# A fourth Strassen product of gate/up in passes, and one main loop over both halves of the tokens

## The chip, the cores and the metric

The kernel runs on one core of one Trainium2 chip. The time is the device time of one execution in microseconds. TensorE (PE) multiplies, VectorE (DVE), ScalarE (ACT) and GpSimd (POOL) work on elements, and nearly all DMAs are issued in order by SyncE (SP).

## The reference, cut to what matters

One decoder block on 2048 tokens of 1024 channels in float32: attention and pooling with their projections, then a SwiGLU network of inner width 2816. The change concerns the network alone:

```python
h = rmsnorm(x, g_ffn_pre) * (1.0 + scale_f) + shift_f            # (2048, 1024)
f = (jax.nn.silu(h @ w_gate) * (h @ w_up)) @ w_down              # w_gate, w_up: (1024, 2816), w_down: (2816, 1024)
x = x + gate_f * rmsnorm(f, g_ffn_post)
```

## The kernel before, in words

**The arithmetic.** A float32 matrix is split into a high and a low fp32r part, and a product is three matmuls, high·high, low·high and high·low (`mm3`, L66 to L73). The split is a cast on ACT, and a subtraction on DVE (`split`, L59). `split_by_bank` (L1170) has ACT copy the rounded part into a PSUM bank as well, so that DVE's subtraction reads one operand from PSUM and one from SBUF.

**Strassen-Winograd outside.** The 2048 tokens are two halves, sb 0 and 1, of 1024. Within a half, h is a 2 by 2 matrix of blocks (512 channels by 512 tokens), and each of w_gate and w_up is, for each j of 11, a 2 by 2 matrix of 512 by 128 blocks (columns j and j+11). Seven products of block sums take the place of eight. One outer product, for one weight (g or u), one half and one j, is a *step* of 12 matmuls of 512 columns: four slices of channels by three.

**Passes.** Three of the seven products (`NQ = 3`) are computed earlier, in passes. A pass q takes 11 values of j; `inner(q, j)` (L1318) makes a second Strassen over g and u on the one side and the two halves of the tokens on the other, so that the four outer products (g and u, half 0 and 1) take seven inner products of 6 matmuls, 42 instead of 48. The results go to DRAM (`pd`, L1374). Each of the seven is a step of its own. While a pass runs, a generator writes the operands (sums of token blocks, split) of what comes next, one piece for each step: `second_operands` in pass 1, `third_operands` in pass 2, `main_operands` in pass 3. `down_sums` (L1589), placed by `DOWN_AT`, makes the block sums of w_down meanwhile.

**Main loop.** `gate_up(sb, j, at)` (L1537) makes the other four products of g and of u for one half and one j: 8 steps, a *block*. It reads the earlier products back (`px`), adds them up, applies silu and the multiplication, makes the block sums of the result and stores them (`ga`). `matrix` (L1412) loads the weights, makes their sums on POOL and splits them; it does so for each half anew.

**Down.** `down(sb)` (L1730) is a Strassen-Winograd product of the result with w_down for one half: seven phases of 11 chunks, 12 matmuls each. The last phases finish the rows of the output (`p4_end`, `p3_end`). In half 0 the operands of half 1 are made beside it (`token_operands`).

**The order.** All steps stand in one list, made by `halves` (L1983): three passes, main loop of half 0, down of half 0, main loop of half 1, down of half 1. The loop at its end (L2112) goes through it: for step n it first does what is due `ahead` of steps to come (loads, weight sums), then the matmuls, then what is due after earlier steps (`takes`), then splits for steps to come (`split_up_to`: at most `PAIRS = 6` steps from n on), then one piece of the side generator. Each engine runs its instructions in the order in which they are written here.

PSUM banks rotate: `g_ps` has 5 for the products of the main loop. `ring` holds 5 pairs of split operands, `fx` one more.

Of the kernel before, what the change touches and what calls it, by code (L numbers as in the profile page):

```python
# [9 lines left out]
F32 = mybir.dt.float32  # L10
# [36 lines left out]
def block_kernel(ctx, tc, x, c, w_cond, b_cond, g_mix_pre, g_mix_post, w_in, w_pool,  # L47
# [46 lines left out]
    sd = {kind: dt(f"sd{kind}", [P, 4, TB]) for kind in "gu"}  # L94
# [34 lines left out]
    def modulated_t(pool, new_ps, xs, a, b, name):  # L129

        for half in range(2):
# [4 lines left out]
            h32 = ft("tr", f"{name}_h{half}", (P, 4, P)) if pool is fx else pool.tile([P, 4, P], F32, tag="h32", bufs=8 if pool is op else 4, name=f"{name}_h{half}")  # L136
# [1022 lines left out]
    def operand(name):  # L1159
        used[0] += 1  # L1160
        pool = fx if fx is not None and used[0] % (RB + 1) == 0 else ring
        return [pool.tile([P, TB], F32R, tag=f"w{n}", bufs=1 if pool is fx else RB, name=f"{name}_{n}") for n in "hl"]

    def new_ops(pool, sb, names):
        return {n: (pool.tile([P, HK, TB], F32R, tag=f"{n}h", bufs=1, name=f"{n}h{sb}"),
                    pool.tile([P, HK, TB], F32R, tag=f"{n}l", bufs=1, name=f"{n}l{sb}")) for n in names}

    MAIN = ("t2", "t3", "t1", "b22")
# [132 lines left out]
    class Step:  # L1301
        def __init__(self, pairs, split, mm, take=()):
            self.pairs, self.split, self.mm, self.take, self.ahead = pairs, split, mm, list(take), []

# [13 lines left out]
    def inner(q, j):  # L1318
# [6 lines left out]
        def load():  # L1325
            turn = 0 if m == 1 else (NQ * HF - 2 - m) % 4
            if m == 0:
                st["g"], st["u"], st["s12"], st["s34"] = (t[:, n] for t in raw_pair(ring, name, (P, 2, TB)) for n in range(2))
            else:
                if m == NQ * HF - 1:  # L1330
                    w = opools["0b"].tile([P, 4, TB], F32, tag="y22", bufs=1, name=f"{name}_32")
                else:
                    w = raw_tile(ring if turn > 1 else fx, turn % 2 == 0, name, (P, 2, TB))
                st["g"], st["u"] = w[:, 0], w[:, 1]
            for n, src in (("g", w_gate), ("u", w_up)):
                (nc.scalar if m in (4, 5) else nc.sync).dma_start(st[n].rearrange("p (k n) -> p k n", k=HK), rows_of(src, min(q, 1) * HK, j + q // 2 * HF))
# [36 lines left out]
        def keep(kind, sb, t):  # L1373
            nc.sync.dma_start(pd[sb][:, j, 2 * q + kind, :], t)  # L1374
# [34 lines left out]
        r[0].ahead = [({1: 9, 2: 12}.get(m, 14), load), (5 if m == 1 else 8, s12), (4 if m == 1 else 7, s34)]  # L1409
        return r  # L1410

    def matrix(kind, src, sb, j, at, take):  # L1412

        name = f"{kind}{sb}_{j}"
        st = {}
        turn_back = sb == 1 and at == 0
        SUMS = ("s2", "s3", "s1", "s4")

        def load(i):
            f = j + i * HF  # L1420
            w32 = raw_tile(ring if kind == "g" else fx, i, name, (P, KC, P))
            if turn_back:
                nc.scalar.dma_start(w32.rearrange("p (i k) n -> p i (k n)", i=2), sd[kind][:, 2 * i:2 * i + 2, :])
                st[SUMS[2 * i]], st[SUMS[2 * i + 1]] = (w32[:, k:k + HK, :].rearrange("p k n -> p (k n)") for k in (0, HK))
                return
            nc.sync.dma_start(w32, rows(src)[:, :, f * P:(f + 1) * P])
            st[("a11", "s1")[i]], st[("a12", "a22")[i]] = (w32[:, k:k + HK, :].rearrange("p k n -> p (k n)") for k in (0, HK))

        def load0():
            load(0)  # L1430

        def load1():
            load(1)
# [727 lines left out]
```

## Time and profile before

| what | value |
|---|---|
| median of 3 runs | 2219.2 us (2216.96 to 2219.46) |
| the profiled execution | 2218.68 us, span 2216.9 us |
| PE busy | 2187.9 us of the span |
| granted TensorE clock, mean | 0.997 |
| DMA, mean over the span | 230 GB/s |
| first half's main loop starts | 1302.49 us (first row of `t_g<-t2h,g_s_h`) |
| down of half 0 | 1543.77 to 1753.37 us |
| main loop of half 1 starts | 1753.21 us |
| down of half 1 | 1999.52 to 2209.12 us |

A row of the timeline has start, duration, engine, line, operation, what is written from what, and in brackets how long the engine was idle before it and what ended that. Names come without their numbers: `t_g<-t2h,g_s_h` is a matmul of the main loop, t2's high part with the split sum of w_gate. A matmul of 512 columns is listed with some 0.39 us, while the next one starts 0.23 us after it: they overlap in the pipeline, so starts are to be compared. Rows of the windows view give, for a stretch, how long each engine was busy and with how many instructions, then the granted clock, the busy share of the DMA engines and their GB/s.

### The profile page before, as it was taken

What the parts mean: (1) busy time and instruction counts of PE and PEld (TensorE: products, weight loads), DVE (VectorE), ACT (ScalarE), POOL (GpSimd) and SP (SyncE); (2) the same over time, 40 slices, a digit from 0 to 9 for tenths busy, and PEclk for the clock granted to TensorE, in tenths of its full rate; (3) what the DMA queues carried; (4) which work ended last, traced back from release to release, by engine and by line L of the source; (5) the groups of instructions that cost most, each with busy time, mean ns of one, the idle gap of its engine ahead of it and who ended that gap; (6) DMA issues with size and microseconds to landing.
All of it is one profiled execution on the core that took longest, in us unless ns stands there. A gap on an engine that the chain in (4) does not pass through costs nothing.

```text
span 2216.9 us, 34775 instructions
## 1 busy us (share of the span) xinstructions
PE 2187.9 (99%) x10415; PEld 1809.8 (82%) x10415; DVE 1692.0 (76%) x2555; ACT 1411.6 (64%) x2879; POOL 1241.8 (56%) x1694
## 2 busy tenths in 40 slices
PE   8999999999999999999999999999999999999998
PEld 6888888888888888888888888888888878888887
DVE  7874499999999966557788877878676777876566
ACT  5334599989989855457666666665554556664444
POOL 1352277787779965548888737774120477761003
PEclk9999999999999999999999999999999999999999
DMA  9996886534444456669989877878777888868664
GB/s 316 335 289 211 283 209 183 161 91 119 119 125 114 135 176 195 199 224 303 316 298 324 283 267 240 274 250 285 271 236 215 257 288 275 261 228 311 208 191 150
DMA packets 385000, 510.66 MB, mean 230 GB/s; under 512 B 25190, under 2 KB 223402, under 8 KB 381868
## 3 DMA queue, kind: packets, MB, share of 16 engines
q1 hardware_dynamic: 381676, 504.77, 70.8%
q10 hardware_dynamic: 3136, 3.67, 0.6%
q8 instruction: 83, 1.36, 0.3%
q14 instruction: 105, 0.86, 0.1%
HBM read 345.29 MB, written 163.05 MB: 229 GB/s over the span
## 4 chain that ended last, share of the span: by engine, by line
PE 54%; DVE 2%; issue 1%; POOL 1%; ACT 1%; DMA 1%; DVEq 0%; SPq 0%; POOLq 0%; ACTq 0%
PE dn0p L72 3%; PE dn0p L73 3%; PE dn0p L71 3%; PE dn1p L71 3%; PE dn1p L72 3%; PE dn1p L73 3%; PE t_g L71 2%; PE t_g L72 2%; PE t_g L73 2%; PE t_u L73 2%; PE t_u L72 2%; PE t_u L71 2%; PE mix L71 1%; PE mix L73 1%; PE mix L72 1%
## 5 line engine op out<-in xcount | busy, mean ns | idle before, releaser
L953 POOL TENSOR_TENSOR w<-sg,pr 128x512 f32<-128x512 f32 (+2 forms) x320 | 306.3, 957 | 46.4 <-DVE pr L948 15.2
L948 DVE TENSOR_TENSOR_SCAN pr<-pr,carry,begin 128x512 f32<-128x512 f32 x192 | 244.2, 1272 | 0.0
L932 ACT ACTIVATE sg<-z 128x512 f32<-128x512 f32 (+2 forms) x320 | 183.0, 572 | 50.9 <-PE z L930 41.1
L62 DVE TENSOR_TENSOR wtl<-wt,wth 128x512 fp32r<-128x512 f32 (+1 forms) x320 | 189.9, 593 | 17.8 <-ACT wth L61 15.7
L61 ACT CAST wth<-wt 128x512 fp32r<-128x512 f32 (+1 forms) x320 | 181.8, 568 | 10.4 <-PE wt L964 8.0
L934 ACT ACTIVATE pr<-z 128x512 f32<-128x512 f32 (+2 forms) x320 | 182.1, 569 | 0.0
L964 PE MATMUL wt<-ident,w 128*128 128x128 f32 x1088 | 172.3, 273 | 1.5 <-POOL pr L944 1.1
L964 PEld LDWEIGHTS wt<-ident,w 128*128 128x128 f32 x1088 | 134.1, 140 | 32.7 <-POOL pr L944 1.8
L979 PE MATMUL av<-wth,vt 128*128 128x512 f32 (+1 forms) x320 | 126.1, 394 | 0.9 <-ACT o L984 0.8
L71 PE MATMUL dn0p<-w0p_h,g0p_h 128*128 128x512 f32 x308 | 119.8, 389 | 0.0
L72 PE MATMUL dn0p<-w0p_l,g0p_h 128*128 128x512 f32 x308 | 119.8, 389 | 0.0
L73 PE MATMUL dn0p<-w0p_h,g0p_l 128*128 128x512 f32 x308 | 119.8, 389 | 0.0
L929 PE MATMUL z<-kt,qt 128*128 128x512 f32 (+2 forms) x320 | 118.7, 371 | 0.7 <-ACT pr L934 0.6
L980 PE MATMUL av<-wtl,vt 128*128 128x512 f32 (+1 forms) x320 | 117.8, 368 | 1.3 <-DVE wtl L62 1.2
L930 PE MATMUL z<-kt,qt 128*128 128x512 f32 (+2 forms) x320 | 117.0, 366 | 0.0
L71 PE MATMUL dn1p<-w1p_h,g1p_h 128*128 128x512 f32 x292 | 113.6, 389 | 0.0
L72 PE MATMUL dn1p<-w1p_l,g1p_h 128*128 128x512 f32 x292 | 113.6, 389 | 0.0
L73 PE MATMUL dn1p<-w1p_h,g1p_l 128*128 128x512 f32 x292 | 113.6, 389 | 0.0
L945 DVE TENSOR_TENSOR_SCAN pr<-pr,zero,begin 128x128 f32<-128x128 f32 (+3 forms) x128 | 111.3, 872 | 1.7 <-ACT pr L934 1.7
L61 ACT CAST g0p_h<-g0p 128x512 fp32r<-128x512 f32 x77 | 48.0, 623 | 100.6 <-PE dn0p L72 82.8
L62 DVE TENSOR_TENSOR g1p_l<-g1p,g1p_h 128x512 fp32r<-128x512 f32 x73 | 52.6, 721 | 74.4 <-ACT g1p_h L61 73.7
L1567 POOL TENSOR_TENSOR gs<-s,s 128x512 f32<-128x512 f32 x44 | 57.8, 1313 | 92.2 <-DVE s L1557 89.2
(808 smaller groups left out, 7298.0 us busy)
## 6 DMA issues: line engine op xcount, KB each, us to landing
pd<-p_c SPq DMA_DIRECT2D x132, 256.0 KB, 4.7
g<-in_w_gate_dram SPq DMA_DIRECT2D x42, 512.0 KB, 5.2
u<-in_w_up_dram SPq DMA_DIRECT2D x42, 512.0 KB, 5.6
px<-pd SPq DMA_DIRECT2D x11, 1536.0 KB, 9.4
wc<-in_w_cond_dram SPq DMA_DIRECT2D x32, 512.0 KB, 7.6
qt<-qd SPq DMA_DIRECT2D x64, 256.0 KB, 4.1
hs<-h2d SPq DMA_DIRECT2D x60, 256.0 KB, 3.9
kt<-kd SPq DMA_DIRECT2D x96, 128.0 KB, 3.3
```

Source lines behind the costliest of these rows:

```text
L61: nc.scalar.copy(hi, src)
L62: low.tensor_tensor(lo, src, raw(hi), ALU.subtract)
L71: nc.tensor.matmul(ps, lh, rh, start=first and i == 0, stop=False)
L72: nc.tensor.matmul(ps, lh, rl, start=False, stop=False)
L73: nc.tensor.matmul(ps, ll, rh, start=False, stop=last and i == n - 1)
L929: nc.tensor.matmul(z[:, 0:L], qt[:, 0, i * P:(i + 1) * P], keys, start=True, stop=False)
L932: nc.scalar.activation(sg[:, 0:L], z[:, 0:L], AF.Sigmoid, scale=0.125)
L934: nc.scalar.activation(pr[:, 0:L], z[:, 0:L], AF.Sigmoid, scale=-0.125)
L948: nc.vector.tensor_tensor_scan(keys, keys, begin, carry, ALU.mult, ALU.bypass)
L953: nc.gpsimd.tensor_tensor(w[:, 0:L], sg[:, 0:L], pr[:, 1:L + 1], ALU.mult)
L964: nc.tensor.transpose(wt[:, i * P:(i + 1) * P], wss[u][i][:, b * P:(b + 1) * P], ident)
L979: nc.tensor.matmul(av[:, lo0:], vb, wh[:, lo0:], start=first, stop=False)
```

## The change

`NQ` is 4: a fourth outer product, of the sum of the weights' two lower blocks, is computed in a fourth pass. Its weights have to be added first, so that twice as many are loaded, and POOL adds them (`row_sum`). A generator `fourth_operands` makes its token operands in pass 3.

The main loop has three products left for g and for u. It goes over j once: a block is now 12 steps, each of the three products for g and u and for both halves, and half 1 uses the same split weights as half 0. All token operands of half 0 and t2 of half 1 are made in pass 4 (`main_operands`), t3 and b22 of half 1 in the first steps of the loop (`rest_operands`); for that the first block has its steps in another order. The early products come back as four loads of 1 MB for each j (`products_load`), in three buffers.

Down of half 1 follows down of half 0 directly; `switch`, `back`, `token_operands` and the storing of weight sums (`sd`) go. Down loads w for four chunks at once.

```diff
-FT = {"tr": 4, "gs": 3, "u4": 1, "gf": 1, "sr": 4, "s": 6, "u2": 2, "w320": 1, "u3": 2, "w321": 1, "p1": 1, "cu": 2}
-PAIRS, HELD = 6, 4
+FT = {"tr": 1, "gs": 3, "u4": 1, "gf": 1, "sr": 4, "s": 6, "u2": 2, "w320": 1, "u3": 2, "w321": 1, "p1": 1, "cu": 2}
+WIDE = {"tr": 4, "gf": 2, "w320": 2, "w321": 2}
+PAIRS, MAIN_PAIRS, HELD = 6, 4, 4
-NQ = 3
-DOWN_AT = (10, 22, 34, 46, 58, 82, 106, 130, 156, 176, 196)
+NQ = 4
+DOWN_AT = (10, 26, 42, 58, 74, 106, 130, 156, 172, 188, 204)
...
+            k0, f = ((0, j), (HK, j), (HK, j + HF), (0, j + HF))[q]
...
+            if q == 3:
...
+                    w = raw_tile(ring, 1, f"{name}_2", (P, 2, TB))
+                    st["g2"], st["u2nd"] = w[:, 0], w[:, 1]
+                for n, src in (("g2", w_gate), ("u2nd", w_up)):
+                    nc.sync.dma_start(st[n].rearrange("p (k n) -> p k n", k=HK), rows_of(src, HK, f))
+
+        def row_sum(n, other):
+            nc.gpsimd.tensor_tensor(st[n], st[n], st[other], ALU.add)
...
+        if q == 3:
+            r[0].ahead += [(10, lambda: row_sum("g", "g2")), (9, lambda: row_sum("u", "u2nd"))]
...
+    def products_load(n, sb, j):
+
+        tag, pool = (("yah", "0r"), ("yal", "0r"), ("y22", "0b"))[next(px_turn) % 3]
+        px[n, sb, j] = opools[pool].tile([P, 4, TB], F32, tag=tag, bufs=1, name=f"px{n}{sb}_{j}")
+        nc.sync.dma_start(px[n, sb, j], pd[sb][:, j, 4 * n:4 * n + 4])
...
+        def take_p6(kind, sb, ps):
+            p1, p2 = to_bank(0, kind, 0, sb), first(0, kind, 1, sb)
+            u2 = st["u2", kind, sb] = ft("u2" if kind == "g" else "u3", f"u2{kind}{sb}_{j}")
+            nc.vector.tensor_tensor(u2, ps, first(0, kind, 0, sb), ALU.add)
+            if kind == "g":
+                gate("a11", sb, "sr", p1, p2)
+            else:
+                up("a11", sb, p1, p2)
...
+            r = Step(int(make), (lambda: split_w(n)) if make else (lambda: None), mm,
+                     [(late, lambda: after(kind, sb, st["ps", n, kind, sb]))])
+            r.cap, r.takes_first, r.pair = MAIN_PAIRS, True, (n, kind)
+            return r
+
+        order = [(n, sb) for n in ("s2", "s3", "s4") for sb in range(2)]
+        if not at:
+            order = [("s2", 0), ("s2", 1), ("s3", 0), ("s4", 0), ("s3", 1), ("s4", 1)]
+        order = [(n, kind, sb) for n, sb in order for kind in "gu"]
...
     def rest_operands():
 
-        ops["b22"] = pair_of(opools["0"], "ya", "b22")
...
+        ops[1].update({n: pair_of(opools["0b"], tag, f"{n}_1") for n, tag in (("t3", "v14"), ("b22", "v32"))})
...
+        for k in range(HK + 2):
+            if k < HK:
+                nc.gpsimd.tensor_tensor(b12[k], b22[k], b12[k], ALU.subtract)
+            for n, raw, i in (("t3", b12, k - 1), ("b22", b22, k - 2)):
+                if 0 <= i < HK:
+                    put(ops[1][n], slice(i * P, (i + 1) * P), raw[i], split if n == "b22" else split_by_bank)
             yield
...
                 def load_w():
-                    ph["w", j] = t = ft("tr", f"w{name}")
-                    nc.sync.dma_start(t, src[:, j, :])
+                    m = min(4, HF - held - j)
+                    k = next(w_turn) % 3
...
+                    nc.sync.dma_start(t[:, 0:m], src[:, j:j + m, :])
...
-                s.ahead.append((5, load_w))
+                if j % 4 == 0:
+                    s.ahead.append((8 if begin else 5, load_w))
...
-            at[(second_operands, third_operands, main_operands)[q]] = len(r)
+            at[(second_operands, third_operands, fourth_operands, main_operands)[q]] = len(r)
...
+        for j in range(HF):
+            s = gate_up(j, j)
...
         for sb in range(2):
-            for n in range(HF):
-                s = gate_up(sb, (n - 1) % HF if sb else n, n)
...
             d = down(sb, lambda sb=sb: pools[sb])
...
-        while split_to < len(steps) and sum(s.pairs for s in steps[n:split_to + 1]) <= PAIRS:
+        while split_to < len(steps) and sum(s.pairs for s in steps[max(0, n - 12):split_to + 1] if s.last >= n) <= steps[split_to].cap:
```

Three places show how instructions move. On PE, where down of half 0 ends: `dn0p3` is the last phase of half 0, `w0p3` and `g0p3` its operands, `t2_g1_10` the first product of half 1's main loop, `dn1p1` the first phase of down of half 1. Before:

```order
L71 MATMUL dn0p3_3_21359<-w0p3_10_h_21607,g0p3_10_h_21603 128x512
L72 MATMUL dn0p3_3_21359<-w0p3_10_l_21608,g0p3_10_h_21603 128x512
L73 MATMUL dn0p3_3_21359<-w0p3_10_h_21607,g0p3_10_l_21604 128x512
L71 MATMUL t2_g1_10_21673<-t2h1_19634,g1_10_s2_h_21628 128x512
L72 MATMUL t2_g1_10_21673<-t2l1_19635,g1_10_s2_h_21628 128x512
L73 MATMUL t2_g1_10_21673<-t2h1_19634,g1_10_s2_l_21629 128x512
```

And now:

```order
L72 MATMUL dn0p3_3_23427<-w0p3_10_h_23665,g0p3_10_h_23661 128x512
L73 MATMUL dn0p3_3_23427<-w0p3_10_l_23666,g0p3_10_h_23661 128x512
L74 MATMUL dn0p3_3_23427<-w0p3_10_h_23665,g0p3_10_l_23662 128x512
L72 MATMUL dn1p1_0_23734<-w1p1_0_h_23692,g1p1_0_h_23688 128x512
L73 MATMUL dn1p1_0_23734<-w1p1_0_l_23693,g1p1_0_h_23688 128x512
L74 MATMUL dn1p1_0_23734<-w1p1_0_h_23692,g1p1_0_l_23689 128x512
```

The turn from down to a main loop is gone; down meets down.

On DVE, in the middle of a block of the main loop: rows with `_l` are splits of weights, `u2`, `u3`, `u4` are sums of products, `s` the gated results. Before, block j=5 of half 0:

```order
L1457 TENSOR_TENSOR u2g0_5_18303<-t2_g0_5_18254,px0_5_18012 128x512
L1542 TENSOR_TENSOR s0_5_00_18305<-p0g0_5_18244,px0_5_18012 128x512
L1182 TENSOR_TENSOR u0_5_s1_l_18308<-u0_5_s1_18193,rounded_18310 128x512
L1457 TENSOR_TENSOR u3g0_5_18333<-t3_g0_5_18289,u2g0_5_18303 128x512
L1542 TENSOR_TENSOR s0_5_10_18335<-p2g0_5_18283,u3g0_5_18333 128x512
L1182 TENSOR_TENSOR u0_5_s4_l_18338<-u0_5_s4_18218,rounded_18340 128x512
L1457 TENSOR_TENSOR u4g0_5_18359<-t1_g0_5_18315,u2g0_5_18303 128x512
L1542 TENSOR_TENSOR s0_5_11_18361<-t1_g0_5_18315,u3g0_5_18333 128x512
L1182 TENSOR_TENSOR g0_6_s2_l_18364<-g0_6_s2_18285,rounded_18366 128x512
```

And now, block j=5, with `t20`, `t21` the products of half 0 and 1:

```order
L1490 TENSOR_TENSOR u2g0_5_20023<-t20_g_5_19981,px00_5_19792 128x512
L1478 TENSOR_TENSOR sa110_5_20025<-b0g0_5_20021,px00_5_19792 128x512
L1490 TENSOR_TENSOR u2u0_5_20047<-t20_u_5_20007,px00_5_19792 128x512
L1482 TENSOR_TENSOR b0u0_5_20045<-b0u0_5_20045,px00_5_19792 128x512
L1483 TENSOR_TENSOR sa110_5_20025<-sa110_5_20025,b0u0_5_20045 128x512
L1490 TENSOR_TENSOR u2g1_5_20067<-t21_g_5_20030,px01_5_19847 128x512
L1478 TENSOR_TENSOR sa111_5_20069<-b0g1_5_20065,px01_5_19847 128x512
L1177 TENSOR_TENSOR g_5_s4_l_20072<-g_5_s4_19877,rounded_20074 128x512
L1490 TENSOR_TENSOR u2u1_5_20099<-t21_u_5_20051,px01_5_19847 128x512
L1482 TENSOR_TENSOR b0u1_5_20097<-b0u1_5_20097,px01_5_19847 128x512
L1483 TENSOR_TENSOR sa111_5_20069<-sa111_5_20069,b0u1_5_20097 128x512
L1177 TENSOR_TENSOR u_5_s4_l_20104<-u_5_s4_19911,rounded_20106 128x512
```

Before, every third row here is a split of weights; now one in six, and what stands between adds up products. From one `u2g0_5` to the next `u2g0_6` it was 26 rows for 8 steps, and is 40 rows for 12.

On POOL, in the last pass: `p3_5` and `p4_5` are j=5 of the pass, `s12` and `s34` the inner sums of its weights, `hs` the token sums made beside it, `wd` those of w_down. Before, pass 3:

```order
L1348 TENSOR_TENSOR p3_5_s12_16217<-p3_5_321_16111 128x256
L1349 TENSOR_TENSOR p3_5_s12_16217<-p3_5_s12_16217,p3_5_321_16111 128x256
L1353 TENSOR_TENSOR p3_5_s34_16237<-p3_5_321_16111 128x256
L1354 TENSOR_TENSOR p3_5_s34_16237<-p3_5_321_16111,p3_5_s12_16217 128x256
L1586 TENSOR_TENSOR wd9_512_16149<-wd20_512_16153,wd9_512_16149 128x512
```

And now, pass 4:

```order
L1342 TENSOR_TENSOR p4_5_320_17373<-p4_5_320_17373,p4_5_2_321_17376 128x512 x2
L1354 TENSOR_TENSOR p4_5_s12_17515<-p4_5_320_17373 128x256
L1355 TENSOR_TENSOR p4_5_s12_17515<-p4_5_s12_17515,p4_5_320_17373 128x256
L1356 TENSOR_TENSOR p4_5_s34_17529<-p4_5_320_17373 128x256
L1357 TENSOR_TENSOR p4_5_s34_17529<-p4_5_320_17373,p4_5_s12_17515 128x256
L1685 TENSOR_TENSOR hs0_3_1_17471<-hs0_3_3_17473,hs0_3_1_17471 128x512
L1685 TENSOR_TENSOR hs0_3_0_17493<-hs0_3_1_17471,hs0_3_0_17493 128x512
```

Two sums of 512 columns stand ahead of the inner sums, and none of w_down's are left beside them.

More of the change, by code (lines that the diff above doesn't have):

```diff
@@ L1688, in main_operands @@
         for i in range(HK):
-            cols = slice(i * P, (i + 1) * P)
-            done, coming = [], list(order) if i + 1 < HK else []
-            sums = itertools.islice(combine(nc.gpsimd, raw[i, 0], raw[i, 1], None, raw[i, 3]), 3)
-            for at, (n, t) in enumerate(itertools.chain(sums, [(None, None)] * 2)):
-                if done:
-                    put(*done.pop(), split_by_bank)
-                if n:
-                    done.append((ops[n], cols, t))
-                if at > 1 and coming:
-                    load(i + 1, coming.pop(0))
+            now = nxt
```

383 lines of the change are left out of this document (179 added, 204 removed).

## The prediction, made before the result was known

> **What bounds the kernel now.** I read the page first: the engines' shares, the slices, and the chain that ended last.
>
> ```profile
> PE 2187.9 (99%) x10415; PEld 1809.8 (82%) x10415; DVE 1692.0 (76%) x2555; ACT 1411.6 (64%) x2879; POOL 1241.8 (56%) x1694
> ...
> PE   8999999999999999999999999999999999999998
> ...
> PE 54%; DVE 2%; issue 1%; POOL 1%; ACT 1%; DMA 1%; DVEq 0%; SPq 0%; POOLq 0%; ACTq 0%
> ```
>
> PE is busy in every slice, and more than half of the chain is PE; nothing else has over 2%. But busy time hides small losses where matmuls overlap, so I went to the timeline, PE's rows in the first main loop, and compared starts.
>
> ```profile
> 1312.01 0.39 PE L71 MATMUL t_u<-t2h,u_s_h 128*128 128x512 f32 x1
> ...
> 1319.94 0.39 PE L73 MATMUL t_u<-t1h,u_s_l 128*128 128x512 f32 x1
> ```
>
> These are the first and last of 36 matmuls: 7.93 us over 35 distances, 0.2266 us each. A step of 12 is 2.72 us, a block of 8 steps 21.76 us. So a matmul saved is worth 0.2266 us, not the 0.39 us of its row. Then I looked for stretches in which starts are further apart. In the network there is one: the turn from down of half 0 to the main loop of half 1.
>
> ```profile
> 1753.21 0.39 PE L71 MATMUL t_g<-t2h,g_s_h 128*128 128x512 f32 x1
> ...
> 1784.04 0.47 PE L71 MATMUL b_g<-b22h,g_s_h 128*128 128x512 f32 x1 [0.75 <-DVE s L1557]
> ...
> 1801.97 0.57 PE L71 MATMUL t_g<-t2h,g_s_h 128*128 128x512 f32 x1 [3.76 <-DVE s L1542]
> ...
> 1814.56 0.39 PE L71 MATMUL t_u<-t2h,u_s_h 128*128 128x512 f32 x1
> ```
>
> The first row starts a block and the last one stands two and a half blocks later: 61.35 us against 2.5 x 21.76 = 54.40, so **6.95 us** are lost here. What PE waits for is DVE (in brackets), which is late with the products' sums. The windows of the main loop and of down quoted further on have PE busy throughout: the network is bound by PE, and DVE is the engine next to it. How near, the first main loop shows, where DVE starts late and catches up.
>
> ```profile
> 1304.98 0.39 PE L73 MATMUL t_g<-t2h,g_s_l 128*128 128x512 f32 x1
> ...
> 1308.24 0.69 DVE L1457 TENSOR_TENSOR u2g<-t_g,px 128x512 f32<-128x512 f32 x1
> ...
> 1314.50 0.39 PE L73 MATMUL t_u<-t2h,u_s_l 128*128 128x512 f32 x1
> ...
> 1320.17 0.39 PE L71 MATMUL b_g<-b22h,g_s_h 128*128 128x512 f32 x1
> 1320.83 0.50 PE L72 MATMUL b_g<-b22l,g_s_h 128*128 128x512 f32 x1 [0.27 <-DVE b22l L1182]
> ...
> 1322.97 0.68 DVE L1457 TENSOR_TENSOR u2u<-t_u,px 128x512 f32<-128x512 f32 x1
> ...
> 1334.67 0.68 DVE L1457 TENSOR_TENSOR u2g<-t_g,px 128x512 f32<-128x512 f32 x1
> ...
> 1439.07 0.68 DVE L1457 TENSOR_TENSOR u2g<-t_g,px 128x512 f32<-128x512 f32 x1
> ```
>
> A product whose last matmul ends at 1305.37 (1304.98 + 0.39) is taken at 1308.24: a lag of 2.9 us. The next such pair has 8.1 us (1314.89 to 1322.97); meanwhile PE loses 0.4 us (two starts 0.66 apart). The last two rows are five blocks apart, 104.40 us: 20.88 us a block while DVE is behind, against PE's 21.76. Its 26 instructions of a block, with their waits for ACT, take 96% of PE's time. That is the margin to watch.
>
> **The change part by part.** *Fewer matmuls.* A pass computes for one j in 42 matmuls what the main loop does in 48. A fourth pass of 11 values of j saves 66; the matmuls of the built kernel are 66 fewer. 66 x 0.2266 = **-14.95 us**.
>
> *The turn goes.* No main loop follows down of half 0 any more, so the 6.95 us have no place: **-6.95 us**. What is late next is asked at the two new seams below.
>
> *The fourth pass.* A j takes 42 x 0.2266 = 9.52 us. POOL has two sums of 512 and four of 256 columns for it, and 16 token sums of 512 in all 11.
>
> ```profile
> L1586 POOL TENSOR_TENSOR wd<-wd,wd 128x512 f32<-128x512 f32 x22 | 28.4, 1296 | 0.6
> ...
> L1348 POOL TENSOR_TENSOR p_s<-p 128x256 f32<-128x256 f32 x19 | 14.2, 745 | 10.4 <-DVE p_s_l L1182 10.4
> ...
> 1000.00:1104.00 104.00, 102.91 (x457) 85.06 (x456) 78.33 (x131) 74.08 (x143) 87.72 (x97) 1.00 0.94 311
> 1326.00:1541.00 215.00, 215.00 (x950) 178.11 (x949) 169.51 (x266) 137.13 (x241) 144.20 (x113) 1.00 0.78 259
> ```
>
> 2 x 1.30 + 4 x 0.745 + 16 x 1.30 / 11 = 7.5 us, 79% of 9.52; in the first pass POOL is busy 87.7 of 104 us and PE loses little. The weights' second half has one buffer, so that load and sums alternate: 5.5 us to land (row of `p<-in_w_up` below) and 2.6 us of sums make 8.1 us, under 9.52. I take 0; had a load the 7.9 us of the larger row below, 10.5 us would cost 11 x 1.0 = 11 us.
>
> *The main loop.* A block is 12 steps, 32.64 us. DVE has 40 instructions in it. At the pace of the old loop's catching up (20.88 / 26 = 0.803 us each, waits included) they take 32.1 us, 98%. Most of those waits were for ACT's rounded copies, of which there are now 6 in 40 rows and not 8 in 26, so I expect nearer 30. I take 0 for the steady loop. POOL has 16 sums, 16 x 1.30 = 20.8 us of 32.64. DMA: 2 MB of weights, four products' loads of 1 MB and 14 stores of 256 KB are 9.96 million bytes, 305 GB/s; the first window above ran at 311 with a share of 0.94.
>
> *The seam into the main loop.* The new first block has twice the splits of token operands, 8 against 4. From its third step to its eighth I count 31 DVE instructions, 31 x 0.685 = 21.2 us (its rows have 0.68 and 0.69), in 6 x 2.72 = 16.3 us: the lag grows by 4.9 us. If it enters with the old 2.9 us, it reaches 7.8, and some more with waits for ACT. A product may wait four steps, 10.9 us, for its bank is written again by the fifth product after it; at the old turn the loss came at such lags. The nearest rows are the old start of this loop (8.1 us of lag, 0.4 us lost) and the turn (6.95). I take **+1.5 us**, ends 0 and 6.95.
>
> *The seam between the down stages.* Half 0's last rows are finished beside the first splits of half 1. Inside down the same stands between its last two phases, and the row of that stretch has PE busy throughout:
>
> ```profile
> 1706.00:1753.00 47.00, 47.00 (x209) 38.91 (x209) 36.03 (x50) 25.74 (x51) 18.02 (x15) 1.00 0.83 263
> 1753.00:1815.00 62.00, 57.44 (x244) 46.50 (x243) 45.90 (x70) 33.05 (x61) 42.09 (x35) 0.97 0.84 269
> ...
> 1734.57 1.74 POOL L1836 TENSOR_TENSOR y_v<-y_v,gf 128x512 f32<-128x512 f32 x1
> 1735.09 1.78 DVE L62 TENSOR_TENSOR g0p_l<-g0p,g0p_h 128x512 fp32r<-128x512 f32 x1
> 1736.79 0.68 DVE L62 TENSOR_TENSOR w0p_l<-w0p,w0p_h 128x512 fp32r<-128x512 f32 x1
> ```
>
> A split that meets a POOL sum takes 1.78 us in place of 0.68. Four rows with two POOL operations each could cost DVE 8 x 1.1 = 8.8 us there. The stretch above has just these and loses nothing, since splits run two chunks (5.4 us) ahead. I take 0, ends 0 and 6.95 (what the turn lost). The Trainium skill, "SBUF — State Buffer", section "SBUF: two separate sides", says that a VectorE operation with two SBUF inputs and a GpSimd operation lock each other out of a shared pair of ports, the later one for all of the other's time. That rule speaks against this change, which takes the finishing of rows from beside sums that read PSUM to beside splits that read SBUF twice; by it alone the seam would cost DVE the 8.8 us, by the row of the stretch they are covered.
>
> *Larger loads in down.* Four chunks of w come in one load of 1 MB, asked for five chunks ahead.
>
> ```profile
> px<-pd SPq DMA_DIRECT2D x11, 1024.0 KB, 7.9
> ...
> p<-in_w_up_dram SPq DMA_DIRECT2D x31, 256.0 KB, 5.5
> ```
>
> Landing after 7.9 us it meets the split, due three steps (8.2 us) later, and PE two steps after that: 0, with at most some tenths of a us in each of 14 phases.
>
> **The sum** on the profiled execution's 2218.68: -14.95 - 6.95 + 1.5 = 2198.28; that execution lies 0.5 us below the median of the runs, so **2198.8 us**.
>
> **The rivals.** *A seam takes the turn's place.* DVE's lag at the start of the new main loop, or the locked splits between the down stages, stop PE as the turn did. For it: the two counts above; against it: the old start of the loop and the old phase boundary. One seam at the turn's price in place of my 1.5: 2204.2; both: 2211.2.
>
> *DVE becomes the bound of the main loop*, the one that ends slower. Its place is the steady block: if 40 instructions need more than 32.64 us, PE waits in each of 11 blocks. In the stretch of the turn DVE did 70 instructions in 62 us, 0.886 each; at that pace 40 take 35.4 us, 2.8 too many, 11 x 2.8 = 30.8 us, 2228 us. It is slower than before from 35.0 us a block (26 us lost). For it: 96% in the old loop, 98% by the same pace; against it: fewer splits with their waits for ACT.
>
> *DMA becomes the bound of the main loop.* If it gave no more than the old loop's 259 GB/s, a block would take 9.96 / 0.259 = 38.5 us, 11 x 5.8 = 64 us more, 2261. Against it: 311 GB/s in the first pass with 102.91 of 104 us of PE.
>
> *The pass doesn't give what it should*, since load and sum of its weights alternate in one buffer: 11 us as worked out, 2209.8.
>
> **How the numbers follow.** My forecast has 0.60, a seam 0.17, DVE 0.13, DMA 0.06, the slow pass 0.04. The range takes in the forecast with both ends of its unknown costs, the seams and the slow pass: from 2194.5 (no new loss, 2197.3, less the 2.2 us by which the fastest run lies under the median, and a little) to 2211.5 (both seams). It leaves out what DVE or DMA would cost, 0.19. About 0.2%, 4.4 us, is what a measurement of this kernel can tell from no change. Faster by more is the forecast, the seams, the slow pass and a quarter of the DVE and DMA cases: 0.86; within it 0.05; slower 0.09, the rest of DVE and DMA.
>
> **What would show it.** Right: 66 matmuls fewer, starts 0.2266 us apart through passes and main loop, no bracket at the start of `dn1p`, and a lag of `u2g` after its product that falls from block to block. Wrong in the seam: brackets on PE naming DVE in the first block of the loop, or a gap within 30 us after down of half 0. Wrong in the loop: blocks over 32.64 us apart with a lag that stays near 10 us (DVE), or `u2` rows idle until `px` lands, and a DMA share near 1 (DMA). Wrong in the pass: `p4` steps over 9.52 us apart for one j, POOL idle until the weights land.

## The result and the profile after

| | before | after |
| --- | --- | --- |
| median of the runs, us | 2219.33 (4 runs, 2216.96 to 2219.46) | 2233.64 (4 runs, 2231.36 to 2235.74) |
| profiled execution, us | 2218.68 | 2234.14 |
| its span, us | 2216.9 | 2232.4 |

The kernel became slower: the ratio is 1.0067, with a 95% interval of 1.0049 to 1.0084. The forecast was 2198.8, with a range up to 2211.5.

The page of the kernel after has these lines in the places of those shown before: busy time by engine, PE's 40 slices, and the chain that ended last.

```profile
PE 2180.1 (98%) x10349; PEld 1794.5 (80%) x10349; DVE 1669.8 (75%) x2552; ACT 1356.4 (61%) x2796; POOL 1217.4 (55%) x1700
...
PE   8999999999999999999999998799999999999998
...
PE 45%; DMA 4%; DVE 4%; POOL 2%; issue 2%; ACT 2%; SPq 0%; DVEq 0%; POOLq 0%; ACTq 0%
```

The 66 matmuls are gone (10415 to 10349). But PE's slices have a dent in the middle, and the chain, which was 54% PE and 1% DMA, is now 45% PE and 4% DMA. The windows give the dent a place: busy time of PE, PEld, DVE, ACT and POOL, then the granted clock, the DMA share and GB/s.

```profile
1305.00:1431.00 126.00, 111.65 (x466) 86.42 (x464) 82.25 (x136) 67.61 (x127) 78.28 (x80) 0.99 0.72 233
1431.00:1476.00 45.00, 35.62 (x148) 28.75 (x149) 28.16 (x46) 23.40 (x41) 19.82 (x16) 0.89 0.85 297
1476.00:1803.00 327.00, 326.92 (x1443) 270.36 (x1442) 262.95 (x411) 159.52 (x283) 197.65 (x156) 1.00 0.94 310
```

The first row is the fourth pass, the second the first block of the main loop, the third its ten other blocks. By starts of matmuls the stages took:

| stage | at PE's pace | after | lost |
| --- | --- | --- | --- |
| passes 1 to 3 | 317.74 (as before the change) | 322.09 | 4.35 |
| pass 4, 11 x 9.52 | 104.7 | 125.7 | 21.0 |
| first block of the main loop, with a step left over from the pass | 34.0 | 45.3 | 11.3 |
| ten further blocks of 32.64 | 326.4 | 326.8 | 0.4 |
| down of half 0, to the first matmul of half 1 | 209.4 | 209.4 | 0.0 |
| down of half 1, to its last matmul | 209.2 | 211.5 | 2.3 |

The losses are 39.3 us in all. Against them stand 14.95 for the matmuls, 6.95 for the turn, 0.4 that the old start of the loop had lost, and 1.3 by which the part ahead of the passes happened to be shorter; that leaves 15.7, and the two executions are 15.5 apart. So both gains came as worked out. No engine is short of time: in pass 4 DVE is busy 82 of 126 us, POOL 78, DMA 0.72. Something stands. The view of waits for 1306 to 1420 (who stood, for whom; us in total, times, longest) names the waits.

```profile
DVE p_c L1384 <- DMA pd<-p_c: 26.5, 9, 5.3
...
POOL p L1342 <- DMA p<-in_w_up_dram: 10.5, 4, 6.0
...
PEld ap L72 <- ACT rounded L1176: 9.7, 7, 2.3
```

SP's waits are an answer of their own, in the same window:

```profile
SPq L1339 <- POOL p L1342: 33.8, 8, 6.5
```

SP issues nearly all transfers, one after the other, and stands 33.8 us in front of the second weights' loads (L1339) until POOL's row sums (L1342) free the one buffer. Behind these loads in SP are the stores of products (L1380), and DVE stands 26.5 us at `p_c`, which needs a buffer that a store has to empty. SP's timeline shows one turn:

```profile
1341.22 0.38 SPq L1339 DMA_DIRECT2D p<-in_w_gate_dram  x1
1341.65 0.50 SPq L1339 DMA_DIRECT2D p<-in_w_up_dram  x1
...
1346.96 0.63 SPq L1615 DMA_DIRECT2D hs<-h2d  x1
1354.16 0.38 SPq L1339 DMA_DIRECT2D p<-in_w_gate_dram  x1
...
1355.18 0.86 SPq L1380 DMA_DIRECT2D pd<-p_c  x2
...
1359.59 0.67 SPq L1339 DMA_DIRECT2D p<-in_w_up_dram  x1
...
1366.30 0.38 SPq L1339 DMA_DIRECT2D p<-in_w_gate_dram  x1
```

From 1347.59 to 1354.16 SP issues nothing. In that time POOL waits for weights, sums, and so lets SP go on:

```profile
1352.86 1.28 POOL L1342 TENSOR_TENSOR p<-p,p 128x512 f32<-128x512 f32 x1 [2.56 <-DMA p<-in_w_up_dram]
...
1364.97 1.31 POOL L1342 TENSOR_TENSOR p<-p,p 128x512 f32<-128x512 f32 x1 [1.44 <-DMA p<-in_w_up_dram]
```

One j takes 12.1 us (1354.16 to 1366.30): 5.4 us pass between the two loads in SP's queue, since stores and other loads stand between them, 5.4 us until the second has landed (1364.97), 1.3 us of sum. The forecast had 8.1 for the same loop, with both loads going out at once. In the kernel's text they stand one right after the other (L1338 and L1339); the rows of SP show that the built program has SP's transfers in an order of its own. So what is said further up, that each engine runs its instructions in the order in which they are written, doesn't hold for SP.

The first block's loss is one gap. DVE's and PE's rows there:

```profile
1441.24 0.69 DVE L1478 TENSOR_TENSOR sa<-b0g,px 128x512 f32<-128x512 f32 x1
1452.06 0.69 DVE L1384 TENSOR_TENSOR p_c<-dp,u4p 128x512 f32<-128x512 f32 x1 [10.13 <-DMA pd<-p_c]
...
1452.90 0.77 PE L72 MATMUL t_g<-t_0h,g_s_h 128*128 128x512 f32 x1 [9.11 <-DVE p_c L1384]
```

and SP's:

```profile
1432.43 4.88 SPq L1380 DMA_DIRECT2D pd<-p_c  x1
1437.36 6.27 SPq L1615 DMA_DIRECT2D hs<-h2d  x5
...
1444.79 1.66 SPq L1380 DMA_DIRECT2D pd<-p_c  x1
```

`rest_operands` takes four of the six `s` buffers for token parts just when the last products of the pass need them; its loads stand in SP until stores have emptied these buffers, the next store stands behind the loads, and DVE stands 10.13 us for that store.

### The profile page after: what moved, and what is told of

It reads as the page before. It is cut to its first block, busy times and chain, and to the rows that moved or that the text cites. A ratio compares the mean times of both kernels' runs of the same rounds, so it can differ in the third digit from the quotient of the medians.

```text
span 2232.4 us, 34290 instructions
## 1 busy us (share of the span) xinstructions
PE 2180.1 (98%) x10349; PEld 1794.5 (80%) x10349; DVE 1669.8 (75%) x2552; ACT 1356.4 (61%) x2796; POOL 1217.4 (55%) x1700
## 4 chain that ended last, share of the span: by engine, by line
PE 45%; DMA 4%; DVE 4%; POOL 2%; issue 2%; ACT 2%; SPq 0%; DVEq 0%; POOLq 0%; ACTq 0%
PE dn0p L72 3%; PE dn0p L74 3%; PE dn0p L73 3%; DMA pd<-p_c 3%; PE dn1p L73 2%; PE dn1p L74 2%; PE dn1p L72 2%; PE t_u L74 2%; PE t_u L73 2%; PE t_u L72 2%; PE t_g L73 2%; PE t_g L72 2%; PE t_g L74 2%; PE mix L72 1%; PE mix L74 1%
## 5 line engine op out<-in xcount | busy, mean ns | idle before, releaser
L1479 ACT ACTIVATE sa<-sa 128x512 f32<-128x512 f32 x88 | 54.9, 633 | 166.0 <-DVE sa L1478 162.6
L63 DVE TENSOR_TENSOR g0p_l<-g0p,g0p_h 128x512 fp32r<-128x512 f32 x77 | 59.3, 771 | 80.0 <-ACT g0p_h L62 80.0
```

What stands on the lines that cost most here:

```text
L63: low.tensor_tensor(lo, src, raw(hi), ALU.subtract)
```

## The experiments

Times are of the profiled execution of each kernel unless a ratio is given; stages are by starts of matmuls, as in the table above. Where nothing else is said, the edit is made to the kernel after the change. A time without a ratio is that of one execution; ten executions of e10 span 2211.86 to 2218.39 us and five of e17 2204.18 to 2214.36, so single executions don't tell totals apart that differ by a few us.

**Three ways at the one buffer.** *e1_sums_apart*: the row sum reads the first weights twice, so that no sum waits for a second load and no second load for a sum. Loads and sums remain; the block sum of the weights is left out, so its products are not those that are wanted.

```
-            nc.gpsimd.tensor_tensor(st[n], st[n], st[other], ALU.add)
+            nc.gpsimd.tensor_tensor(st[n], st[n], st[n], ALU.add)
```

> As the change, but POOL's two sums of a j in pass 4 add a tile to itself and read nothing of the second half of the weights, which is still loaded: the same loads, the same sums, no load that waits for a sum (the block sum of the weights is left out). Theory (the one buffer: the load waits for the sums, SP waits in front of it, and the stores of products behind it come late): pass 4 goes from 125.8 us to 105 to 108 us; the first block of the main loop from 45.3 to 34 to 38 us; in all 2200 to 2208 us. Rival (pass 4 has too much DMA traffic or too much POOL work): pass 4 stays at 120 us or more, in all 2228 us or more.

*e2_pool_queue*: the loads go out from POOL's queue, behind POOL's own sums.

```
-                    nc.sync.dma_start(st[n].rearrange("p (k n) -> p k n", k=HK), rows_of(src, HK, f))
+                    nc.gpsimd.dma_start(st[n].rearrange("p (k n) -> p k n", k=HK), rows_of(src, HK, f))
```

> As the change, but the second half of pass 4's weights is asked for from POOL's queue, behind the sum that frees the buffer, and not from SP's. Theory (what costs is SP standing in front of that load while stores of products wait behind it, and the two loads being torn apart by other DMAs): pass 4 at 106 to 114 us, in all 2203 to 2218 us. Rival (the latency of load and sum in one buffer is itself too long, whoever issues): pass 4 stays near 125 us.

*e3_split_wait*: the buffer is taken once for the whole pass, so that the load of g waits for the sum of g alone.

```
+    second = {}
...
-                    w = raw_tile(ring, 1, f"{name}_2", (P, 2, TB))
+                    w = second.setdefault(0, None)
+                    if w is None:
+                        w = second[0] = raw_tile(ring, 1, f"{name}_2", (P, 2, TB))
```

> As the change, but the one buffer of the second weights is taken once for the whole pass, so that each of its two halves is loaded as soon as its own sum is done, and not both sums. Theory: the loop for one half is 5.3 us of load and 1.3 us of sum, SP stands shorter; pass 4 at 106 to 118 us, in all 2203 to 2222 us. Rival (traffic or POOL's work): pass 4 stays at 120 us or more.

| | us | pass 4 | first block |
| --- | --- | --- | --- |
| after | 2234.14 | 125.7 | 45.3 |
| e1_sums_apart | 2223.91 | 114.4 | 46.4 |
| e2_pool_queue | 2221.39 | 111.7 | 46.8 |
| e3_split_wait | 2230.46 | 121.2 | 46.0 |

With the same bytes, e1 saves 11.3 us of pass 4 and e2 14.1: what the loads stand for, and whose queue they stand in, costs more than what they carry. Splitting the wait in two gives only 4.5, for SP still stands (36.3 us in its view of waits, 33.8 before). e2 came where its expectation had the pass, e1 and e3 did not (e3's 121.2 is what its rival had), and all missed their expected totals: the first block kept its loss, which I had not seen as a cause of its own. The Trainium skill, "DMA: Bandwidth & Descriptors", section "Rules for kernel authors", says that spreading transfers over several issuing engines doesn't help bandwidth and saves only issue time. By that alone e2 should have won little. Its 12.8 us are not bandwidth: the DMA share was 0.72 in the pass it mends. They are the waits of others behind a load that cannot start, and the loads go out together again: in e2 0.76 us apart, and the loop takes 9.92 us.

```profile
1335.28 0.76 POOL L1339 DMA_DIRECT2D p<-in_w_gate_dram  x1 [0.29 <-POOL p L1342]
1336.04 0.75 POOL L1339 DMA_DIRECT2D p<-in_w_up_dram  x1
...
1345.20 0.76 POOL L1339 DMA_DIRECT2D p<-in_w_gate_dram  x1 [0.29 <-POOL p L1342]
```

What bounds that loop now is POOL's own work: it is busy 9.45 of these 9.92 us, with two row sums, four block sums, two token sums and two issues, and waits for no other engine in it. The loop stays at 9.8 to 9.9 us for five j in a row, over PE's 9.52. What follows is the same fault once more: SP stands up to 9.6 us for a buffer that POOL's token sums free, the first weights stand behind that, and POOL stands 4.6 us for them.

**The stores, and the buffers of the first block.** *e4_stores_act* takes the stores out of SP's queue, *e5_both_queues* does so and has the loads on POOL's, *e8_sr_tags* changes two buffers in `rest_operands` only, and *e9_all_three* does all of it.

```
-            nc.sync.dma_start(pd[sb][:, j, q // 2 * 4 + 2 * kind + q % 2, :], t)
+            nc.scalar.dma_start(pd[sb][:, j, q // 2 * 4 + 2 * kind + q % 2, :], t)
```

```
-        b12 = [token_part(1, NTS, "s", i) for i in range(HK)]
+        b12 = [token_part(1, NTS, tag, i) for i, tag in enumerate(("sr", "sr", "s", "s"))]
```

> The stores of the passes' products (L1380) are issued from ACT's queue, all else as after the change. Theory (SP serves its queue in order, and what stands behind a load that waits for a buffer is late: stores, and so the six `s` buffers, and so DVE): DVE's waits for `pd<-p_c` go (26.5 us from 1306 to 1420 before), the weights' own loop of 12.1 us a j stays; pass 4 falls from 125.8 to 115-122 us, the first block of the main loop from 45.3 to 36-41, the whole to 2218-2228. Rival (the DMA engines are full there, whichever queue issues): pass 4 stays at 123 or more, the block at 44 or more, 2230-2236.

> The second weights' loads (L1339) from POOL's queue, as before, and the products' stores (L1380) from ACT's. Theory: nothing that waits for POOL's sums stands ahead of the stores any more; pass 4 106-111 us (111.7 with the loads alone moved, 104.7 at PE's pace), first block of the main loop 36-41 (46.8), the whole 2205-2214. Rival (what is left after the loads were moved is DMA traffic or DVE's splits): 2218-2224, block 45 or more.

> Two of the four loads of token parts at the start of the main loop go to `sr` buffers in place of `s`, so that four `s` buffers in place of two are left for the last products; all else as after the change. Theory (the first block's 11.3 us are DVE standing at `p_c` for a buffer whose store is behind these loads): first block 45.3 to 35-40, pass 4 as it is, 122-128, the whole 2225-2230. Rival (the block loses its time to the twice as many splits on DVE, as I counted in the prediction, or to the loads of products): block 44-47, 2232-2237.

> All three edits together: second weights' loads from POOL's queue, stores from ACT's, two token parts in `sr`. Theory: pass 4 105-111, first block 34-38, the whole 2202-2211, faster than before by 0.4 to 0.8%. Rival (traffic or DVE): 2217 or more, no faster than before.

| | us | passes 1 to 3 | pass 4 | first block |
| --- | --- | --- | --- | --- |
| e4_stores_act | 2276.76 | 377.1 | 118.0 | 38.3 |
| e5_both_queues | 2267.53 | 378.0 | 112.0 | 37.2 |
| e8_sr_tags | 2225.07 | 320.9 | 125.7 | 38.4 |
| e9_all_three | 2264.13 median, 1.0204 [1.0187, 1.0222] | 375.6 | 113.5 | 34.0 |

In pass 4 and the first block e4 did what the theory said (118.0 and 38.3). But it lost 55 us in the passes ahead, which neither theory had. The waits of e4_stores_act from 1000 to 1300 show ACT standing for transfers that have nothing to do with its work (first fence), and its timeline shows a store in front (second):

```profile
ACT p_s_h L1169 <- DMA tdt<-wd: 10.6, 2, 5.5
```

```profile
1048.67 0.34 ACTq L1380 DMA_DIRECT2D pd<-p_c  x1
1049.05 0.62 ACT L1169 CAST p_s_h<-p_s 128x512 fp32r<-128x512 f32 x1 [5.47 <-DMA tdt<-wd]
```

The cast reads `p_s`, which POOL made; ACT stood 5.47 us ahead of it because the store ahead of it on ACT waited until `tdt<-wd`, a store on SP's queue, had landed. The built program says why: each transfer waits on a counter that an earlier one, of SP's queue or ACT's, has used, as in two rows of ACT (`DMAHW1_49` and `DMAHW3_49` are such counters, `DVE_49` counts DVE's instructions):

```
1501 L1380 DMA pd_159<-p_4_c_13674 128x512 [waits DMAHW1_49,DVE_49]
1505 L1380 DMA pd_158<-p_5_c_13692 128x512 [waits DMAHW3_49,DVE_49]
```

On SP such a wait holds up only the transfers behind it; on ACT it holds up the casts and copies as well that the passes need. e8 is the clean test of the first block: 45.3 to 38.4 us, pass 4 untouched, and the total 9.1 us lower (2.3 of it in down of half 1, which ran without its loss; the rest, small differences in the parts ahead, nearly cancels). Together with the faster pass in e9 the block ran at PE's pace, 34.0 us: the doubled splits on DVE cost nothing there. In pass 4 itself e5 and e9 (112.0 and 113.5) missed their expectations, 106 to 111 and 105 to 111: with the loads on POOL's queue, moving the stores away from SP gave the pass nothing more than e2 had.

**What is left, and what causes it.** *e10_two_fixes* joins e2 and e8, *e11_later_loads* asks later for what SP stood in front of, *e12_old_spacing* puts back the old `DOWN_AT`, and *e13_no_second* has neither second loads nor row sums, with e8's tags: its pass 4 multiplies by the first weights alone.

```
-            for n, k, tag in zip((1, 3, 0), (6, 6, 5), tags):
+            for n, k, tag in zip((1, 3, 0), (4, 4, 3), tags):
...
-        at_ = (21, 20, 17, 11, 13, 12, 5, 4, 8, 3) if not at else (13, 12, 11, 12, 8, 7, 6, 5, 4, 3)
+        at_ = (16, 15, 14, 11, 11, 10, 5, 4, 8, 3) if not at else (13, 12, 11, 12, 8, 7, 6, 5, 4, 3)
```

> Second weights' loads from POOL's queue and two token parts in `sr`, stores left on SP. If the two losses are apart from each other: 2221.39 (loads alone moved) less the 7 us that the tags gave in the first block, less the 1 to 2 us in the second down stage: 2211-2215, pass 4 109-114 us, first block 37-40. Rival (the gain in the block only moves to the next wait, since pass 4's stores are still late): 2218-2222.

> As e10_two_fixes, and what SP stood in front of is asked for later: the token parts of the main loop two steps later, the first block's weights five steps later (g) to three (u). Theory (SP's wait in front of loads whose buffers are not yet free is what is left of pass 4's loss, since the products' stores are queued behind): pass 4 105-109 us, the whole 2206-2211. Rival (the loads then come too late themselves, POOL and ACT wait for them at the start of the main loop): first block 42 or more, the whole 2214-2222.

> The steps at which down's weights are summed (DOWN_AT) as before the change, all else as after it. Theory (the 4.2 us lost in passes 2 and 3 come from the new spacing): passes 1 to 3 take 318 us again, in place of 322.1, the whole 2228-2231. Rival (they come from the token operands of the second and third pass, which have one buffer fewer to load into, `tr` 1 for 4): 321-323, the whole 2231-2236.

> The fourth pass without its second weights (neither loads nor the two row sums; its products are of the first weights alone), and two token parts in `sr`. Theory (pass 4 loses its 21 us by the one buffer, the queue behind its loads and POOL's two more sums): pass 4 105-109 us, first block 37-40, the whole 2203-2210. Rival (the pass is slow because of its token sums and what else is loaded for the main loop): pass 4 115 or more, 2214-2225.

| | us | passes 1 to 3 | pass 4 | first block |
| --- | --- | --- | --- | --- |
| e10_two_fixes | 2214.78 median, 0.9984 [0.9974, 0.9993] | 321.2 | 111.4 | 40.1 |
| e11_later_loads | 2216.09 | 322.6 | 111.6 | 40.7 |
| e12_old_spacing | 2233.06 | 321.6 | 123.5 | 46.6 |
| e13_no_second | 2201.95 | 322.7 | 104.7 | 34.0 |

e13 settles where the loss is from. Its windows over pass 4 and the first block have PE busy throughout:

```profile
1306.00:1411.00 105.00, 105.00 (x465) 86.95 (x464) 83.86 (x137) 67.91 (x127) 51.60 (x57) 1.00 0.72 232
1411.00:1445.00 34.00, 34.00 (x152) 28.15 (x151) 29.19 (x46) 23.24 (x41) 18.97 (x15) 1.00 0.97 336
```

The token sums, the products' stores, px and the splits are all in it. So the second weights, by their loads, their sums and the order in which they stand, cost pass 4 its 21 us; none of the rest does. e11 doesn't test what it was meant to test: the trace has SP's transfers in the same order as e10's but for one load of a token part, so later asking in the text was not later asking in the program, and the time stayed. The old spacing gave passes 1 to 3 back only 0.5 of 4.3 us.

**The time of asking, and the sums.** Loads 16 steps ahead and sums 10 and 9 ahead, with 7 steps to a j, leave in the text no step between a sum and the next load in the same buffer. *e15_asked_later* and *e16_asked_latest* make room there. *e14_dma_adds* lets the transfer add. *e17_one_sum_dve* and *e18_sums_dve* start from e10 and move sums to DVE.

```
(e15, on e8; second() issues the two loads of the second weights)
-            r[0].ahead += [(10, lambda: row_sum("g", "g2")), (9, lambda: row_sum("u", "u2nd"))]
+            r[0].ahead += [(9, lambda: row_sum("g", "g2")), (9, lambda: row_sum("u", "u2nd"))]
+            r[0].ahead.insert(1, (13, second))
(e14, on e8)
+            nc.gpsimd.dma_start(st[n].rearrange("p (k n) -> p k n", k=HK), rows_of(src, HK, j + HF), accum_op=ALU.add)
(e17, on e10; e18 has nc.vector for both)
-            nc.gpsimd.tensor_tensor(st[n], st[n], st[other], ALU.add)
+            (nc.gpsimd if n == "g" else nc.vector).tensor_tensor(st[n], st[n], st[other], ALU.add)
```

> The second weights are added to the first by the transfer itself (a DMA that accumulates, issued from POOL's queue 12 steps ahead): no second buffer, no row sums; and two token parts in `sr`. Theory (alternation in one buffer and POOL's two more sums cost pass 4 its 21 us, as the 104.7 us without them show): if an accumulating transfer lands about as fast as a plain one (5.3 us for 256 KB), pass 4 takes 105-108 us, the first block 34-38, the whole 2201-2208, faster than before by 0.5 to 0.8%. Rival (POOL stands at the issue until the first weights have landed, or the accumulating transfer lands much later, 10 us and more): pass 4 115 or more, the whole 2214-2230.

> As e8_sr_tags (2225.07, pass 4 125.7 us), but the second weights are loaded 13 steps ahead in place of 16, and summed 9 and 9 steps ahead in place of 10 and 9; queue SP, bytes and sums as before. Theory (no slack between the last sum and the next load in the order written, so SP stands and everything behind it is late): with 3 steps, 4.1 us, of slack SP's wait at these loads falls from 33.8 us to under 15, pass 4 takes 106-116 us, the whole 2206-2216. Rival (POOL and the queues are too full, whenever it is asked): pass 4 120 or more, 2219-2228.

> As e15_asked_later, but loads 12 steps ahead, sums 9 and 8, the block sums 7 and 6 ahead in place of 8 and 7. Theory: as e15, 2204-2216, better than e15 if SP's standing rules, worse if the landing (5.3 us) now meets the sums. Rival: 2219-2228.

> As e10_two_fixes (2214.78 us; pass 4 111.4), with the row sum of u on DVE in place of POOL. If POOL's fullness is what is left: pass 4 105-108, the whole 2207-2211. If it is SP in front of the main loop's loads, or DVE has no room for 11 more sums (81.65 of 111 us busy, a sum 0.7 to 1.8 us): 110-114, 2213-2218.

> As e17_one_sum_dve, with both row sums on DVE. If POOL's fullness is what is left: pass 4 105-108, the whole 2205-2211, though DVE then has 22 more instructions (15 to 39 us). If not: 111-118, 2215-2222.

| | median us | ratio to before | passes 1 to 3 | pass 4 | first block |
| --- | --- | --- | --- | --- | --- |
| e14_dma_adds | 2252.25 | 1.0151 [1.0134, 1.0168] | 320.8 | 150.5 | 41.0 |
| e15_asked_later | 2224.24 | 1.0021 [1.0011, 1.0031] | 320.8 | 123.0 | 37.9 |
| e16_asked_latest | 2228.95 (one run) | | 322.3 | 126.9 | 38.5 |
| e17_one_sum_dve | 2208.71 | 0.9957 [0.9942, 0.9972] | 323.4 | 109.5 | 34.4 |
| e18_sums_dve | 2213.12 | 0.9977 [0.9967, 0.9987] | 325.1 | 111.5 | 37.2 |

The theory of the missing slack was not tested. The traces of e8 and e15 have SP's transfers in the same order up to 1376 us, which is eight of the eleven j: the room made in the text didn't reach the program (e16 differs from e8 there by one load of a token part). SP still stands 28.5 us in front of these loads in e15, and pass 4 is 2.7 us shorter, not 10. Whether slack in SP's own order would help stays open. With the loads in SP's queue it is 118 us or more in every variant that has to wait for both sums or one (e3, e4, e8, e12, e15, e16); on POOL's, with the sums kept, 109.5 to 113.5, wherever the stores go. In e14 POOL takes the place of SP, as its rival had it, though its 150.5 and 2252 us lie far past that rival's range: it issues the adding transfer late, behind its other work, and then stands for it.

```profile
1335.50 1.76 POOL L1334 DMA_DIRECT2D p<-in_w_up_dram  x1
1345.98 0.73 POOL L1346 TENSOR_TENSOR p_s<-p 128x256 f32<-128x256 f32 x1 [8.73 <-DMA p<-in_w_up_dram]
```

10.5 us from issue to use, against 5.4 for the plain load, in a chain in which nothing of the next j is started before: up to 16.7 us from one issue to the next, 13.7 in the mean of the 11 j. Whether more room ahead would hide it was not tried.

e17 is faster than before and after alike. Its windows over the stretches of pass 4 and the first block:

```profile
1306.00:1411.00 105.00, 101.56 (x444) 82.64 (x443) 87.74 (x142) 67.89 (x127) 76.53 (x85) 1.00 0.88 275
1411.00:1445.00 34.00, 33.89 (x150) 27.75 (x149) 27.57 (x40) 19.43 (x34) 16.78 (x14) 1.00 0.94 317
```

POOL, which in e2 was busy 89.03 of these 105 us, has 76.53; SP's wait for POOL's token sums, 20.5 us in e10 from 1306 to 1420, is 7.7; the first block takes 34.4 us. So more than half of what e10 had left over PE's pace in the two stages, 7.6 of 12.8 us, went when POOL had less to do, in the block (40.1 to 34.4) more than in the pass (111.4 to 109.5). The pass is still 4.8 us over PE's pace, and passes 1 to 3 are 2.2 us longer than in e10; neither was followed up. With both sums on DVE (e18) POOL stands 31.8 us for DVE's sums before it may issue the next loads, and part of the gain is given back. e17's total lies where full POOL as the cause had it, its pass 4 between the two expectations; e18's pass 4 came where the other account had it, its total in neither range.

## Why the prediction was wrong

*Fewer matmuls* and *the turn goes*: right, with their sizes. In ten blocks of the main loop 0.4 us are lost, in down of half 0 nothing, and nothing at the border of the two down stages.

*DVE or DMA as the bound of the main loop* (0.13 and 0.06): neither came. From the third block on blocks are 32.64 us apart (the second took 33.04), with DVE busy 262.95 of 327 us, about 80%, and the DMA share 0.94 at 310 GB/s.

*The fourth pass*: this is the step that failed. The prediction put it: "The weights' second half has one buffer, so that load and sums alternate: 5.5 us to land (row of `p<-in_w_up` below) and 2.6 us of sums make 8.1 us, under 9.52. I take 0". The rival stood there at 0.04 and 11 us. The loop was 12.1 us where I looked, since the load of u goes out 5.4 us after that of g. I had counted landing and sums as if SP were free; the larger fault is that I costed the buffer for its own loop only, and did not ask what is queued behind the waiting load on SP. Behind it were the stores that free DVE's buffers. It cost 21.0 us where I took 0 and the rival 11, and without the second weights it is 0 (e13). Taking the waits between load and sum away gave 11.3 us (e1), taking the loads out of SP's queue 14.1 (e2). My 7.5 us of POOL's work for a j was a mean that spread 16 token sums over 11 j; where two fall on a j it is 2.6 + 3.0 + 2.6 = 8.2 us, and with the two issues on POOL the loop was 9.92 (e2). "`p4` steps over 9.52 us apart for one j, POOL idle until the weights land" was the sign I had named, and it is what the trace shows. I had also let the rivals come one at a time: time slower than before was given to DVE and DMA alone, and a slow pass together with a slow seam had no chance of its own.

*The seam into the main loop*, +1.5 with ends 0 and 6.95: the loss is 11.3 and its cause another. I had counted DVE's doubled splits; with the buffers and the pass put right the block runs at 34.0 us with the same splits (e9, e13). What cost was `rest_operands` taking four of six `s` buffers ahead of the last products, and SP's order (e8: 6.9 of the 11.3), on top of a pass that was late already (the rest: 40.1 in e10, 34.4 in e17).

*The seam between the down stages*, 0: right, as PE's rows at the border and the next split on DVE that met a POOL sum show.

```profile
2012.59 0.39 PE L74 MATMUL dn0p<-w0p_h,g0p_l 128*128 128x512 f32 x1
2012.82 0.39 PE L72 MATMUL dn1p<-w1p_h,g1p_h 128*128 128x512 f32 x1
...
2023.36 1.78 DVE L63 TENSOR_TENSOR w1p_l<-w1p,w1p_h 128x512 fp32r<-128x512 f32 x1
```

The splits do take 1.78 us there, as the rule that I weighed has it, and they are covered, as the row of the old phase boundary had it.

*The passes 1 to 3*, not in my sum: 4.3 us. In the chain of waits of after, from 1108 to 1136, a landing `pd<-p_c` is 55.3%: stores again. The spacing of down's sums accounts for 0.5 us of it at most (e12, one execution). Its rival there, fewer buffers for the token parts of the next passes, was not run by itself. From 1284 to 1306 POOL's sums of down's weights and the first second weights are in the chain. Which of the parts of the change does it was not settled; each kernel with the change has 3.0 us or more there, e17 5.7 and e18 7.4.

*Larger loads in down*, 0: 2.3 us lost once in half 1, and none in e8, e9 or e17. The trace of after names not the large load of w but that of g: ACT's cast of `g1p` stood 5.52 us for it (to 2042.82), and SP, which issues it, had stood from 2028.69 to 2033.31 in front of a load of `x1b` until an operation of POOL (`cr`) was done. So it looks like a load behind one that waits once more; no run tests it.

Of the 35.9 us by which the profiled execution missed the sum of 2198.28, pass 4 is 21.0, the seam 9.8 (11.3 less 1.5), passes 1 to 3 4.3, down of half 1 2.3, less 1.3 at the start: 36.1, which is 0.2 more than there is to explain.

## What to carry to other kernels

A load that waits for its buffer is not charged to that buffer alone: list what stands behind it on the queue that issues it, and which engine's buffers those transfers free. Where one buffer serves a load and a sum in turn, count the loop with all that the queue puts between, and put such a load on the queue of the engine that frees the buffer if that engine has the time; here that took 14 us from the pass. Read the order of a queue from the trace, not from the kernel's text: in e11, e15 and e16 loads were asked for two to five steps later in the text, and SP's order hardly changed. Before stores go to a computing engine's queue, look what they will wait for: with 176 stores on ACT the kernel was 43 us slower.

## What the runs showed of the hardware that was not expected

- ACT stood 5.47 us behind a store of its own queue that waited for a transfer of SP's queue whose data it doesn't touch (e4). The counters that the built program hands to transfers in turn tie the two queues together.
- A load issued from POOL takes 0.75 to 0.76 us of POOL, the adding one 1.25 to 1.83, where SP's rows for plain loads of these weights mostly have 0.38 to 0.5. Two of them for each j are 1.5 of 9.52 us, which counts on an engine that is busy 85% (POOL in e2).
- After PE had stood 9.11 us, the next matmuls started 0.57 and then six times 0.43 us apart in place of 0.2266, which is 1.5 of the 11.3 us of that block. The granted clock was 1.00 from 1436 to 1443, 0.50 from 1452 to 1456 and 1.00 from 1457 to 1470:

```profile
1453.47 0.63 PE L73 MATMUL t_g<-t_0l,g_s_h 128*128 128x512 f32 x1
1453.89 0.63 PE L74 MATMUL t_g<-t_0h,g_s_l 128*128 128x512 f32 x1
...
1456.31 0.39 PE L74 MATMUL t_g<-t_0h,g_s_l 128*128 128x512 f32 x1
```

The Trainium skill, "TensorE: Matmul & The Clock Gate", section "Part 1: The HAM clock gate (the "warmup" mystery)", says that the array's clock falls to half after an idle window of about 3.4 us; the rows agree, with 0.43 against 0.2266.
